# A two-block transformer in float32: first stage with x's high parts made by two engines, tile 1's statistics moved ahead of two weight parts, and tile 0's products issued in the order in which their operands are made

## The chip, the core and the metric

The kernel runs on one NeuronCore of a Trainium2 chip. The core has five engines that run apart from one another, each with its own instruction stream, and wait for each other by semaphores: TensorE (PE; its weight loads stand in the profile as PEld) multiplies matrices into PSUM; VectorE (DVE) and ScalarE (ACT) work on tiles in SBUF and PSUM; GpSimd (POOL) does a few small operations; SyncE (SP) issues most DMA transfers. The metric is the time of one execution on the device in microseconds (us), from one launch, with all inputs in the device's memory. Lower is better.

## What is computed

Two transformer blocks on 256 tokens of width 1024, all in float32. The change lies in the first lines of the first block:

```python
h = layer_norm(x, ln0_g, ln0_b)            # 256 x 1024
proj = h @ w_in[l] + b_in[l]               # 1024 x 4352
qa, ka, va, qb, kb, vb, ga, gb = jnp.split(proj, IN_SPLITS, axis=-1)
```

After it come neighbourhood attention and windowed attention, a gated mix, a feed-forward layer, and the second block with pooling, shared-key attention and two convolutional feed-forward layers.

## The kernel before

**Products in three pieces.** To keep float32 accuracy at the matmul's reduced-precision format, each operand is split into a high part (rounded to that format) and a low part (the remainder). A product is then three matmuls: high by high, low weight by high x, high weight by low x.

**Weights.** The class `Weights` streams 512 KB parts from memory in one fixed order. `load` (line 93) lets SyncE issue the transfer of the next part into one of six raw buffers (`wraw`). `high` (120) lets ScalarE write the high part (`whi`, line 134) and returns a function `low`; called, it lets VectorE write the low part (`wlo`, line 144) and then calls `load` for the next transfer, since the raw buffer is free after it. `highs(n)` (149) does n high parts and returns their `low` functions; `pump` (115) does both at once. Seven pairs of buffers hold split parts; `free` (161) gives a pair back.

**The first stage** (lines 505 to 591). The 256 tokens are two tiles of 128, `x_t[0]` and `x_t[1]`. `ln0(t)` (505) normalises a tile: two statistics instructions and their sum, then centring times the gain on VectorE (line 285), then the scaling by the inverse deviation, one half on ScalarE (`times`, line 341) and one on VectorE (514). `fm_banks` (347) transposes the tile with eight matmuls (line 354) into two PSUM banks of four 128-column pieces each. `parts0` (516) adds the layer norm's bias piece by piece and makes x's parts from the banks: eight high pieces `xh` (522), and, when the returned `lows` is called, eight low pieces `xl` (527), all on VectorE.

The first three 256-column units of `w_in` are two parts each, so parts 0 to 5. The class `Tm` multiplies them with the tokens as the stationary operand: `run(0)` (421) takes tile 0 through the three units, 24 matmuls each (line 434): high by high, low weight, low x, over eight pieces of x; the first unit takes the first four pieces of both high and low weight, then the other four, then low x. ScalarE evacuates each unit's sum (`tmc`, 439). Near the end of the last unit, `late` puts tile 1's transposes and its parts into the streams. `run(1)` then takes tile 1 through the same weights, frees them unit by unit, and splits a new part after each of the first two units. `finish` (444) transposes the results back (line 448), and the stages that follow go on with `unit_a` and others (mostly line 375).

**What sets the order.** The order on every engine is the order in which the program writes instructions; the scheduler is off. An engine works through its stream strictly, so an instruction that waits holds back everything behind it. On SyncE the loads stand in the order of the parts and each waits for the `low` that frees its raw buffer. The calls that set the order of the first stage are these:

```python
ln0(0)
bs = fm_banks(x_t[0])
lows = W.highs(2)
x_lows = parts0(bs, 0)
for low in lows:
    low()
x_lows()
```

After them come the transfer of the column constants `cols`, `W.pump(1)` three times (parts 2, 3, 4), `ln0(1)`, and `W.pump(2)` (parts 5, 6).

## Time and profile before

| | us |
|---|---|
| median of the runs shown | 869.26 |
| lowest run | 868.75 |
| the profiled execution | 869.44 |
| its span from the first to the last instruction | 867.7 |
| TensorE busy | 838.6 |
| VectorE busy | 642.3 |
| ScalarE busy | 489.9 |

The profile is of one execution. Its views are a page of totals, a table of chosen stretches of time, a timeline per engine, in which neighbouring instructions of one line are merged into one row (start, time from the first start to the last end, count), and a list of who waited for whom. A matmul's row carries the time until its last result is written, so rows that follow one another overlap; the pace is the distance between starts.

### The profile page before, as it was taken

Reading aid. Unit: us, or ns where it says so; the run is one execution under the profiler, and the core shown is the slowest. Engines: PE = TensorE matmul, PEld = TensorE weight load, DVE = VectorE, ACT = ScalarE, POOL = GpSimd, SP = SyncE. Lnnn points to the kernel's source line nnn. Section 1 sums busy time; section 2 is a strip of 40 time slices with the busy share of each in tenths; the row PEclk is TensorE's granted clock in tenths of the full one; section 3 lists DMA queues with packets and bytes.
Section 4 is the critical chain, followed back from the end, with each engine's and each line's share of the span. In section 5 each row is a group of like instructions: output and inputs, shape, how many; then the busy total and the mean of one; then the engine's idle time right before and its main releaser. Section 6 shows DMA issues by size and latency. Waiting matters only on the chain.

```text
span 867.7 us, 15201 instructions
## 1 busy us (share of the span) xinstructions
PE 838.6 (97%) x5874; PEld 758.8 (87%) x5874; DVE 642.3 (74%) x1145; ACT 489.9 (56%) x904; POOL 73.4 (8%) x97
## 2 busy tenths in 40 slices
PE   7999999999999999979999999999999999999997
PEld 5989889879889999879999999988776999999995
DVE  7575874786828888786799777664896689977772
ACT  3465666444624457455676655555785567665551
POOL 0003000002000000010000000138620000000000
PEclk9999999999999999999999999999999999999999
DMA  8494453558616666523557565434262456756531
GB/s 323 139 306 159 137 204 98 170 179 300 217 65 217 213 218 221 200 98 134 172 188 253 182 215 185 156 126 129 78 210 81 166 178 214 243 197 214 181 114 49
DMA packets 44042, 154.62 MB, mean 178 GB/s; under 512 B 5153, under 2 KB 6049, under 8 KB 43970
## 3 DMA queue, kind: packets, MB, share of 16 engines
q1 hardware_dynamic: 41616, 146.90, 49.6%
q0 software_dynamic: 1632, 5.93, 1.9%
q8 instruction: 46, 0.75, 0.3%
q10 hardware_dynamic: 722, 0.82, 0.3%
q14 instruction: 26, 0.21, 0.1%
HBM read 152.58 MB, written 1.05 MB: 177 GB/s over the span
## 4 chain that ended last, share of the span: by engine, by line
PE 39%; DVE 7%; ACT 6%; DMA 2%; issue 2%; POOL 1%; DVEq 0%; POOLq 0%; ACTq 0%
PE bank_a L375 22%; PE bank_b L375 13%; DVE wlo L144 2%; PE bank_a L434 2%; ACT whi L134 2%; DMA wraw<-wts_dram 2%; ACT p L1335 1%; ACT scr L308 1%; PE bank_a L1356 1%; DVE X L337 1%; DVE cv L1148 1%; POOL rstd L272 1%; PE bank_a L1242 0%; DVE p L741 0%; DVE cv L1146 0%
## 5 line engine op out<-in xcount | busy, mean ns | idle before, releaser
L144 DVE TENSOR_TENSOR wlo<-wraw,whi 128x1024 fp32r<-128x1024 f32 x261 | 312.2, 1225 | 74.3 <-ACT whi L134 73.7
L375 PE MATMUL bank_a<-xh,whi 128*128 128x256 f32 x1056 | 296.0, 280 | 1.9 <-DVE cv L1148 1.7
L375 PE MATMUL bank_a<-xh,wlo 128*128 128x256 f32 x1056 | 292.9, 277 | 0.6 <-DVE wlo L144 0.5
L375 PE MATMUL bank_a<-xl,whi 128*128 128x256 f32 x1056 | 292.8, 277 | 0.0
L134 ACT ACTIVATE whi<-wraw 128x1024 fp32r<-128x1024 f32 x261 | 264.9, 1050 | 19.2 <-DMA wraw<-wts_dram 16.5
L375 PEld LDWEIGHTS bank_a<-xh,whi 128*128 128x128 f32 x1056 | 198.6, 188 | 7.4 <-ACT whi L134 2.7
L375 PEld LDWEIGHTS bank_a<-xl,whi 128*128 128x128 f32 x1056 | 198.6, 188 | 1.7
L375 PEld LDWEIGHTS bank_a<-xh,wlo 128*128 128x128 f32 x1056 | 198.5, 188 | 1.0 <-DVE wlo L144 1.0
L1145 ACT ACTIVATE cv<-bank_a,cols 128x256 f32<-128x256 f32 x76 | 41.9, 558 | 79.0 <-PE bank_a L375 78.9
L375 PE MATMUL bank_b<-wlo,ah 128*128 128x512 f32 x176 | 69.4, 394 | 0.0
L375 PE MATMUL bank_b<-whi,al 128*128 128x512 f32 x176 | 69.0, 392 | 0.0
L375 PE MATMUL bank_b<-whi,ah 128*128 128x512 f32 x176 | 68.5, 389 | 0.0
L1146 DVE SCALAR_TENSOR_TENSOR cv<-bank_a,cols,cv 128x255 f32<-128x255 f32 x76 | 36.5, 480 | 42.1 <-ACT cv L1145 41.9
L375 PE MATMUL bank_b<-wlo,uh 128*128 128x512 f32 x128 | 50.4, 394 | 0.0
L375 PE MATMUL bank_b<-whi,ul 128*128 128x512 f32 x128 | 50.4, 393 | 0.0
L375 PE MATMUL bank_b<-whi,uh 128*128 128x512 f32 x128 | 50.0, 390 | 0.0
L344 ACT ACTIVATE uh<-ur 128x256 fp32r<-128x256 f32 x32 | 13.2, 412 | 59.1 <-DVE ur L942 44.1
L272 POOL TENSOR_TENSOR rstd<-ve,neghalf 128x1 f32<-128x1 f32 x22 | 13.4, 610 | 387.8 <-DVE ve L313 248.2
L921 POOL TENSOR_SCALAR wraw<-wraw,cols 128x256 f32<-128x256 f32 x28 | 29.8, 1082 | 165.8 <-DMA wraw<-wts_dram 162.9
L375 PEld LDWEIGHTS bank_b<-wlo,ah 128*128 128x128 f32 x176 | 33.1, 188 | 6.6
L1148 DVE SCALAR_TENSOR_TENSOR cv<-bank_a,cols,cv 128x254 f32<-128x254 f32 x76 | 36.6, 482 | 2.7
L375 PEld LDWEIGHTS bank_b<-whi,al 128*128 128x128 f32 x176 | 33.1, 188 | 6.3
(207 smaller groups left out, 1267.7 us busy)
## 6 DMA issues: line engine op xcount, KB each, us to landing
wraw<-wts_dram SPq DMA_DIRECT2D x268, 512.0 KB, 4.4
v<-bvec_dram POOLq DMA_DIRECT2D x10, 512.0 KB, 5.3
v<-bvec_dram SPq DMA_DIRECT2D x4, 512.0 KB, 8.0
nab<-nab_dram SPq DMA_DIRECT2D x4, 384.0 KB, 6.3
poolA<-const_dram POOLq DMA_DIRECT2D x1, 544.0 KB, 7.1
scr<-x_dram SPq DMA_DIRECT2D x2, 256.0 KB, 3.1
scr<-x_dram SPq DMA_DIRECT2D x1, 512.0 KB
out_dram<-X SPq DMA_DIRECT2D x2, 256.0 KB, 2.1
```

The lines of the kernel that those rows point to most:

```text
L134: self.nc.scalar.activation(out=hi, in_=r, func=AF.Copy)
L144: (eng or self.nc.vector).tensor_tensor(out=lo, in0=r, in1=hi.bitcast(F32), op=ALU.subtract)
L272: nc.gpsimd.tensor_tensor(out=r, in0=v, in1=neghalf, op=ALU.pow)
L308: nc.scalar.activation(out=junk[:, HALF[q if into is None else into]], in_=src, func=AF.Square, scale=1.0 / 32.0, accum_out=ss[:, q:q + 1])
L337: nc.vector.scalar_tensor_tensor(out=x[:, s], in0=junk[:, s], scalar=r, in1=x[:, s], op0=ALU.mult, op1=ALU.add)
L344: nc.scalar.activation(out=hi, in_=src, func=AF.Copy)
L375: nc.tensor.matmul(o, lhsT=l, rhs=r, start=start and i == 0, stop=stop and i == 2)
L434: nc.tensor.matmul(o[:, :256], lhsT=self.kx(k)[b][:, t * P:(t + 1) * P], rhs=self.cs[u][k // 4][a][:, k % 4, :], start=(i, k) == order[0], ...
L921: nc.gpsimd.tensor_scalar(out=d, in0=d, scalar1=g, scalar2=None, op0=ALU.mult)
L1145: nc.scalar.activation(out=v, in_=o[:, :T], func=AF.Identity, scale=col(c + 2), bias=col(c + 3))
L1146: nc.vector.scalar_tensor_tensor(out=v[:, 1:T], in0=o[:, 0:T - 1], scalar=col(c + 1), in1=v[:, 1:T], op0=ALU.mult, op1=ALU.add)
L1148: nc.vector.scalar_tensor_tensor(out=v[:, 2:T], in0=o[:, 0:T - 2], scalar=col(c), in1=v[:, 2:T], op0=ALU.mult, op1=ALU.add)
```

## The change

In `parts0` the high pieces can now be made by either engine: `act_high` on ScalarE, `high` on VectorE, and `low` on VectorE, each for a half of the pieces (`K0`: pieces 0 to 3, `K1`: 4 to 7). For tile 0 VectorE makes the high pieces of `K0` and ScalarE those of `K1`; for tile 1 it is the other way round. The low parts of the weights and of x alternate on VectorE. Tile 1's statistics come after the low part of weight part 2, ahead of the low part of 3; its centring and scaling come ahead of the low parts of 4 and 5, whose high parts are issued on ScalarE before tile 1's scaling. Tile 0's products are issued by `run0` in groups of four from a list of (unit, half, kind): kind 0 is high by high, 1 low weight, 2 low x. Tile 1's transposes stand ahead of the last two groups. Part 6 is split after them; the transfer of `cols` is issued behind tile 1's scaling and `halfb`, which reads it, later still. The computation is the same; only the order of the additions within a sum differs.

```diff
+            def run0(self, plan):
+                self.cs = [[W.take(4, 256) for _ in range(2)] for _ in range(self.n)]
+                o = [None] * self.n
+                left = [[(h, i) for h in range(2) for i in range(3)] for _ in range(self.n)]
+                for step in plan:
+                    if callable(step):
+                        step()
+                        continue
+                    u, h, i = step
...
+                    for k in range(4):
+                        nc.tensor.matmul(o[u][:, :256], lhsT=self.kx(4 * h + k)[b][:, 0:P],
+                                         rhs=self.cs[u][h][a][:, k, :], start=first and k == 0,
+                                         stop=not left[u] and k == 3)
+                    if not left[u]:
...
+                        nc.scalar.activation(out=self.tm[u][:, 0, :], in_=o[u][:, :256], func=AF.Copy)
...
+            def act_high(ks):
+                for k in ks:
+                    src, c, hi, _ = at(k)
+                    nc.scalar.activation(out=hi, in_=src, func=AF.Identity, bias=c)
...
         ln0(0)
-        bs = fm_banks(x_t[0])
-        lows = W.highs(2)
-        x_lows = parts0(bs, 0)
-        for low in lows:
-            low()
-        x_lows()
+        w_lows = W.highs(1)
+        act_high, high, low = parts0(fm_banks(x_t[0]), 0)
+        high(K0)
+        act_high(K1)
+        w_lows += W.highs(1)
+        w_lows[0]()
+        low(K0)
+        w_lows[1]()
+        low(K1)
+        w_lows += W.highs(1)
+        w_lows[2]()
+        w_lows += W.highs(1)
+        st = small([P, 2, 6], "bst")
+        for q in range(2):
+            ln_stats(x_t[1], st, q)
+        mr = ln_rstd(st)
+        w_lows[3]()
+        w_lows += W.highs(2)
+        ln_centre(x_t[1], mr, g0, 0)
+        times(x_t[1], mr[1], x_t[1], 0)
+        ln_centre(x_t[1], mr, g0, 1)
...
         nc.scalar.dma_start(out=cols[:, :C_B0], in_=cols_in[:, :C_B0])
-        for _ in range(3):
-            W.pump(1)
-        ln0(1)
-        W.pump(2)
...
-        tm.run(0, late=lambda: parts0(fm_banks(x_t[1]), 1)())
+        t1 = []
+
+        def tile1():
+            t1.extend(parts0(fm_banks(x_t[1]), 1))
+            t1[0](K0)
+            w_lows[4]()
+            w_lows[5]()
+            t1[1](K1)
+            for ks in (K0, K1):
+                t1[2](ks)
...
+        tm.run0([(0, 0, 0), (0, 0, 1), (0, 1, 0), (0, 0, 2), (0, 1, 1), (1, 0, 0), (0, 1, 2), (1, 0, 2), (1, 1, 0),
+                 (1, 1, 2), (1, 0, 1), (2, 0, 0), (2, 0, 2), (1, 1, 1), (2, 1, 0), (2, 1, 2), tile1,
+                 (2, 0, 1), (2, 1, 1)])
+        W.pump(1)
         tm.run(1, (2,))
```

**VectorE, from tile 0's high pieces to tile 1's parts.** Before; the numbers behind names are buffers: `wraw_94`, `96`, `98`, `101`, `103`, `105` are the raw weight parts 0 to 5, `scr_81` is tile 1.

```order
L527 SCALAR_TENSOR_TENSOR xl_116<-bank_a_130,cols_87,xh_115 128x128 x4
L527 SCALAR_TENSOR_TENSOR xl_116<-bank_a_135,cols_87,xh_115 128x128 x4
L144 TENSOR_TENSOR wlo_170<-wraw_98,whi_169 128x1024
L144 TENSOR_TENSOR wlo_176<-wraw_101,whi_175 128x1024
L144 TENSOR_TENSOR wlo_182<-wraw_103,whi_181 128x1024
L297 BN_STATS bst_187<-scr_81 128x6 x2
L278 BN_AGGR mv_190<-bst_187 128x2
L280 TENSOR_SCALAR ve_192<-mv_190 128x1
L285 SCALAR_TENSOR_TENSOR scr_81<-scr_81,mv_190,bank_b_107 128x512
L285 SCALAR_TENSOR_TENSOR scr_81<-scr_81,mv_190,bank_b_108 128x512
L514 TENSOR_SCALAR scr_81<-scr_81,rstd_194 128x512
L144 TENSOR_TENSOR wlo_201<-wraw_105,whi_200 128x1024
```

Now the same stretch, from the low part of weight part 0:

```order
L144 TENSOR_TENSOR wlo_131<-wraw_94,whi_130 128x1024
L555 SCALAR_TENSOR_TENSOR xl_116<-bank_a_133,cols_87,xh_115 128x128 x4
L144 TENSOR_TENSOR wlo_152<-wraw_96,whi_151 128x1024
L555 SCALAR_TENSOR_TENSOR xl_116<-bank_a_138,cols_87,xh_115 128x128 x4
L144 TENSOR_TENSOR wlo_169<-wraw_98,whi_168 128x1024
L297 BN_STATS bst_177<-scr_81 128x6 x2
L278 BN_AGGR mv_180<-bst_177 128x2
L280 TENSOR_SCALAR ve_182<-mv_180 128x1
L144 TENSOR_TENSOR wlo_175<-wraw_101,whi_174 128x1024
L285 SCALAR_TENSOR_TENSOR scr_81<-scr_81,mv_180,bank_b_107 128x512
L285 SCALAR_TENSOR_TENSOR scr_81<-scr_81,mv_180,bank_b_108 128x512
L582 TENSOR_SCALAR scr_81<-scr_81,rstd_184 128x512
```

The statistics of tile 1 (`bst`) stand behind the low part of weight part 2 instead of behind that of 4, and tile 1's centring has the low parts of 0 to 3 ahead of it where it had those of 0 to 4. The low parts of 4 and 5 are the next two rows.

**ScalarE, the same stretch.** Before:

```order
L134 ACTIVATE whi_140<-wraw_94 128x1024
L134 ACTIVATE whi_143<-wraw_96 128x1024
L538 DMA cols_87<-cols_dram 128x440
L134 ACTIVATE whi_169<-wraw_98 128x1024
L134 ACTIVATE whi_175<-wraw_101 128x1024
L134 ACTIVATE whi_181<-wraw_103 128x1024
L341 ACTIVATE scr_81<-scr_81,rstd_194 128x512
L134 ACTIVATE whi_200<-wraw_105 128x1024
L134 ACTIVATE whi_206<-wraw_155 128x1024
```

and now:

```order
L134 ACTIVATE whi_130<-wraw_94 128x1024
L545 ACTIVATE xh_115<-bank_a_138,cols_87 128x128 x4
L134 ACTIVATE whi_151<-wraw_96 128x1024
L134 ACTIVATE whi_168<-wraw_98 128x1024
L134 ACTIVATE whi_174<-wraw_101 128x1024
L134 ACTIVATE whi_189<-wraw_103 128x1024
L134 ACTIVATE whi_192<-wraw_105 128x1024
L341 ACTIVATE scr_81<-scr_81,rstd_184 128x512
L584 DMA cols_87<-cols_dram 128x440
L441 ACTIVATE tmc_230<-bank_a_200 128x256
```

Four high pieces of x stand between the high parts of weight parts 0 and 1. The high part of 5 (`wraw_105`) stood behind tile 1's scaling (`scr_81`) and stands ahead of it; the transfer of `cols` stood behind the high part of 1 and stands behind the scaling.

**TensorE, the second half of tile 0's products and tile 1's transposes.** Before, `whi_169` to `wlo_176` are parts 2 and 3, `181`, `200`, `201` parts 4 and 5:

```order
L434 MATMUL bank_a_241<-whi_175,xh_115 128x256 x4
L434 MATMUL bank_a_241<-wlo_170,xh_115 128x256 x4
L434 MATMUL bank_a_241<-wlo_176,xh_115 128x256 x4
L434 MATMUL bank_a_241<-whi_169,xl_116 128x256 x4
L434 MATMUL bank_a_241<-whi_175,xl_116 128x256 x4
L434 MATMUL bank_a_268<-whi_181,xh_115 128x256 x4
L434 MATMUL bank_a_268<-whi_200,xh_115 128x256 x4
L434 MATMUL bank_a_268<-wlo_182,xh_115 128x256 x4
L434 MATMUL bank_a_268<-wlo_201,xh_115 128x256 x4
L434 MATMUL bank_a_268<-whi_181,xl_116 128x256 x2
L354 MATMUL bank_a_287<-ident_86,scr_81 128x128 x4
L354 MATMUL bank_a_292<-ident_86,scr_81 128x128 x4
```

and now, with `168`, `169`, `174`, `175` for parts 2 and 3 and `189` to `193` for 4 and 5:

```order
L436 MATMUL bank_a_221<-whi_174,xh_115 128x256 x4
L436 MATMUL bank_a_221<-whi_174,xl_116 128x256 x4
L436 MATMUL bank_a_221<-wlo_169,xh_115 128x256 x4
L436 MATMUL bank_a_248<-whi_189,xh_115 128x256 x4
L436 MATMUL bank_a_248<-whi_189,xl_116 128x256 x4
L436 MATMUL bank_a_221<-wlo_175,xh_115 128x256 x4
L436 MATMUL bank_a_248<-whi_192,xh_115 128x256 x4
L436 MATMUL bank_a_248<-whi_192,xl_116 128x256 x4
L354 MATMUL bank_a_271<-ident_86,scr_81 128x128 x4
L354 MATMUL bank_a_276<-ident_86,scr_81 128x128 x4
L436 MATMUL bank_a_248<-wlo_190,xh_115 128x256 x4
L436 MATMUL bank_a_248<-wlo_193,xh_115 128x256 x4
```

The groups with low parts of the third unit's weights stood ahead of tile 1's transposes and are now the only ones behind them; the groups of the second and the third unit take turns.

## Rows read from the trace of the kernel before

**Rows 1.** The page, busy us (share of the span) xinstructions of each engine.

```profile
PE 838.6 (97%) x5874; PEld 758.8 (87%) x5874; DVE 642.3 (74%) x1145; ACT 489.9 (56%) x904; POOL 73.4 (8%) x97
```

**Rows 2.** Stretches: busy us per engine, granted clock, DMA share, GB/s.

```profile
12.00:16.00 4.00, 4.00 (x20) 4.00 (x21) 4.00 (x10) 2.12 (x2) 0.00 (x0) 1.00 1.02 406
...
20.00:22.50 2.50, 0.00 (x0) 0.00 (x0) 1.88 (x4) 1.68 (x3) 0.55 (x1) 1.00 0.78 305
22.50:26.00 3.50, 3.45 (x16) 3.45 (x17) 2.45 (x3) 1.48 (x3) 0.00 (x0) 0.51 0.36 90
26.00:38.00 12.00, 12.00 (x97) 11.43 (x96) 6.68 (x18) 4.20 (x9) 0.00 (x0) 1.00 0.34 113
38.00:50.00 12.00, 12.00 (x83) 10.54 (x82) 7.42 (x10) 7.25 (x14) 0.00 (x0) 1.00 0.79 248
50.00:60.00 10.00, 10.00 (x60) 8.28 (x59) 7.84 (x8) 6.89 (x10) 0.00 (x0) 1.00 0.90 290
```

**Rows 3.** Timeline of TensorE: start us, us, what xcount [idle before <-releaser].

```profile
7.41 1.97 PE L354 MATMUL bank_a<-ident,scr 128*128 128x128 f32 x8 [0.21 <-ACT scr L341]
...
9.29 1.22 PE L434 MATMUL bank_a<-whi,xh 128*128 128x256 f32 x4
...
11.91 1.22 PE L434 MATMUL bank_a<-wlo,xh 128*128 128x256 f32 x4 [1.40 <-DVE wlo L144]
...
22.55 1.22 PE L434 MATMUL bank_a<-whi,xh 128*128 128x256 f32 x4 [3.02 <-ACT whi L134]
...
23.57 1.91 PE L434 MATMUL bank_a<-wlo,xh 128*128 128x256 f32 x8
...
25.27 0.63 PE L434 MATMUL bank_a<-whi,xl 128*128 128x256 f32 x2
...
33.82 1.10 PE L434 MATMUL bank_a<-whi,xh 128*128 128x256 f32 x8
...
36.65 1.07 PE L448 MATMUL bank_a<-ident,tmc 128*128 128x128 f32 x8
```

**Rows 4.** Timeline of VectorE, the same columns.

```profile
8.56 2.16 DVE L522 TENSOR_SCALAR xh<-bank_a,cols 128x128 fp32r<-128x128 f32 x8 [0.77 <-PE bank_a L354]
...
10.63 2.35 DVE L144 TENSOR_TENSOR wlo<-wraw,whi 128x1024 fp32r<-128x1024 f32 x2
...
12.90 2.15 DVE L527 SCALAR_TENSOR_TENSOR xl<-bank_a,cols,xh 128x128 fp32r<-128x128 f32 x8
...
14.97 3.49 DVE L144 TENSOR_TENSOR wlo<-wraw,whi 128x1024 fp32r<-128x1024 f32 x3
...
18.38 1.28 DVE L297 BATCH_NORM_STATS2 bst<-scr 128x6 f32<-128x512 f32 x2
...
20.00 1.39 DVE L285 SCALAR_TENSOR_TENSOR scr<-scr,mv,bank_b 128x512 f32<-128x512 f32 x2
...
21.50 0.49 DVE L514 TENSOR_SCALAR scr<-scr,rstd 128x512 f32<-128x512 f32 x1
```

**Rows 5.** Timeline of ScalarE, the same columns.

```profile
8.17 1.06 ACT L134 ACTIVATE whi<-wraw 128x1024 fp32r<-128x1024 f32 x1 [0.82 <-DMA wraw<-wts_dram]
...
13.21 1.06 ACT L134 ACTIVATE whi<-wraw 128x1024 fp32r<-128x1024 f32 x1 [1.48 <-DMA wraw<-wts_dram]
...
14.87 1.07 ACT L134 ACTIVATE whi<-wraw 128x1024 fp32r<-128x1024 f32 x1 [0.61 <-DMA wraw<-wts_dram]
...
20.82 0.72 ACT L341 ACTIVATE scr<-scr,rstd 128x512 f32<-128x512 f32 x1 [4.88 <-DVE scr L285]
...
37.84 0.85 ACT L565 ACTIVATE fm_ka<-bank_a,cols 128x256 f32<-128x256 f32 x2
...
40.68 0.47 ACT L565 ACTIVATE fm_ka<-bank_a,cols 128x256 f32<-128x256 f32 x1
```

**Rows 6.** SyncE's longest wait to 130 us; a stretch in the middle.

```profile
SPq L100 <- DVE wlo L144: 82.8, 26, 8.5
...
387.00:392.00 5.00, 4.97 (x30) 4.73 (x28) 4.38 (x5) 1.54 (x3) 0.55 (x1) 0.66 0.09 37
```

More of the change, by code (lines that the diff above doesn't have):

```diff
@@ L516, in parts0, with at @@
         def parts0(bs, t):
-            todo = []
-            for k in range(8):
-                src = bs[k // 4][:, k % 4 * P:(k % 4 + 1) * P]
-                hi, lo = (a[:, k, t * P:(t + 1) * P] for a in xT)
-                nc.vector.tensor_scalar(out=hi, in0=src, scalar1=col(C_B0 + k), scalar2=None, op0=ALU.add)
-                todo.append((lo, src, col(C_B0 + k), hi))
-            def lows():
-                for lo, src, c, hi in todo:
+            def at(k):
+                return (bs[k // 4][:, k % 4 * P:(k % 4 + 1) * P], col(C_B0 + k)) + tuple(
+                    a[:, k, t * P:(t + 1) * P] for a in xT)
@@ L527, in lows, with high, low @@
+            def act_high(ks):
+                for k in ks:
+                    src, c, hi, _ = at(k)
+                    nc.scalar.activation(out=hi, in_=src, func=AF.Identity, bias=c)
+            def high(ks):
+                for k in ks:
+                    src, c, hi, _ = at(k)
+                    nc.vector.tensor_scalar(out=hi, in0=src, scalar1=c, scalar2=None, op0=ALU.add)
+            def low(ks):
+                for k in ks:
+                    src, c, hi, lo = at(k)
                     nc.vector.scalar_tensor_tensor(out=lo, in0=src, scalar=c, in1=hi.bitcast(F32), op0=ALU.add,
@@ L528, in lows @@
                                                    op1=ALU.subtract)
[L529 removed]
+            return act_high, high, low
+        K0, K1 = range(4), range(4, 8)
         ln0(0)
[L532 to L537 removed]
+        w_lows = W.highs(1)
[3 more added lines that the diff above has]
+        w_lows += W.highs(1)
@@ new lines, in model @@
+        w_lows[0]()
[14 more added lines that the diff above has]
+        ln_centre(x_t[1], mr, g0, 1)
+        nc.vector.tensor_scalar(out=x_t[1][:, HALF[1]], in0=x_t[1][:, HALF[1]], scalar1=mr[1], scalar2=None,
+                                op0=ALU.mult)
@@ L555, in load_nab @@
             nc.sync.dma_start(out=nab[p], in_=nab_in[p])
-        halfb = few.tile([P, 16], F32, name="halfb")
-        nc.vector.tensor_scalar(out=halfb, in0=cols[:, C_GA:C_GA + 16], scalar1=0.5, scalar2=None, op0=ALU.mult)
         fm = {}
@@ L591, in model @@
         tm.finish(1, qk_epi(("ka0", "ka1"), (C_KA, C_KA + 1)))
+        halfb = few.tile([P, 16], F32, name="halfb")
+        nc.vector.tensor_scalar(out=halfb, in0=cols[:, C_GA:C_GA + 16], scalar1=0.5, scalar2=None, op0=ALU.mult)
         W.pump(1)
```

14 lines of the change are left out of this document (8 added, 6 removed).

## The prediction, made before the changed kernel was run

> **What bounds the kernel now.** I read the page's busy table first: TensorE is busy 97% of the span [rows 1], so time is won only where TensorE waits or runs slowly. The table of stretches shows such a place: no matmul from 20.0 to 22.5, then 3.5 us at a granted clock of 0.51, and from 26 on TensorE busy without a gap through 60 us [rows 2]. TensorE's timeline of the first 38 us gives the waits: 1.40 us until 11.91 for `wlo`, 3.02 us until 22.55 for `whi` [rows 3]. It also gives the pace. Eight products took 1.70 us (23.57 to 25.27), 0.2125 each, where the granted clock is the lower level; 24 took 2.83 us (33.82 to 36.65), 0.118 each, at the upper one. The four products at 11.91 took 1.22 us, just as long as the four at 22.55 under the low clock, although the granted column says 1.00 from 12 to 16 [rows 2]: I trust the pace, and with 20 products in those 4 us (0.2 each, near the lower pace) I read the clock as low until about 15.8. So the stage that ends at 36.65 (the transposes of line 448) holds 144 products and 16 transposes, about 19 us of work at the upper pace, and took from 7.41 to 36.65.
>
> Who is late? VectorE's timeline [rows 4] is a chain without a pause from 8.56 to 21.99: high parts of x, two `wlo`, low parts, three `wlo`, then all of tile 1's layer norm. ScalarE waits behind it: it scales tile 1 at 20.82 and only then turns to `whi` of part 5, which the third unit needs. That turn is the 3.02 us wait.
>
> **The change, step by step.** Everything until 8.56 stays. I walk VectorE's new order with spacings from [rows 4]: an `xh` or `xl` of 128x128 is 0.259 (2.07 us from 12.90 to 14.97 for eight), a `wlo` 1.135 (2.27 us from 10.63 to 12.90 for two), the statistics until the centring 1.62 (18.38 to 20.00), the two centrings 1.50 (20.00 to 21.50), the scaling 0.49.
>
> - Four `xh` from 8.56 to 9.59, `wlo` 0 to 10.73, four `xl` to 11.76, `wlo` 1 to 12.90, four `xl` to 13.93, `wlo` 2 to 15.07.
> - Statistics to 16.69, `wlo` 3 to 17.82, centring to 19.32, scaling to 19.81, `wlo` 4 to 20.95, and `wlo` 5, now the last part that the stage needs, ends 1.23 later at 22.18.
>
> ScalarE must keep ahead of that chain. `whi` 0 runs 8.17 to 9.23 [rows 5]; the transposes end at 9.38 [rows 3]; then come its four `xh`, an operation of this size that the trace doesn't have on ScalarE. The nearest row is the 128x256 one with a bias: two took 0.85, one 0.47 [rows 5], 0.38 apart. Bounds are 0.19 (half the columns, half the time) and 0.38 (no less for fewer columns); I take 0.26, taking off 128 columns at the pace of `whi` (1.06 us for 1024, 0.12). Four end at 9.43 + 1.04 = 10.47, `whi` 1 at 11.53, ahead of 11.76 when VectorE wants it. At 0.38 it ends at 12.01: 0.25 us late. At 0.19 nothing changes, since VectorE decides.
>
> One sentence of the Trainium skill speaks against this edit: the page "ScalarE: Activation LUTs", section "Rules for kernel authors", gives adds to VectorE rather than ScalarE, and its section "What ACT_TABLE_LOAD costs" prices an activation with a pointer bias at about 280 ns + 0.833 ns a column with some 93 ns of overlap, an estimated 0.29 apart for 128 columns. By the page's price `whi` 1 would end at about 11.65, still in time, and the sum would be the same; no row of before has that size.
>
> The later weights are no limit: part 3 landed at 13.21 and part 4 at 14.87 [rows 5] and are wanted at 16.69 and 19.81. Part 5 has no row; at 406 GB/s [rows 2] its 0.524 MB takes 1.3 us behind part 4, so `whi` 5 ends near 17.3, wanted at 20.95. The `cols` transfer, now issued behind tile 1's scaling at about 19.3, is wanted by `halfb` and the bias reads near 30.
>
> TensorE then. After the first four products (over by 10.5) it waits for `wlo` 0 until 10.79, and from there the groups of four stand in the order in which parts arrive. At the lower pace a group is 0.85, at the upper one 0.47. With the rise at 15.8 the six groups from 10.79 reach 15.8 and the next ten and eight transposes about 21.1; each group's data is older than its turn (`xl` at 13.93 for a group at 15; `wlo` 3 at 17.88 for one at 18.8; tile 1 scaled by 19.81 for transposes from 20.2). `wlo` 4 lets four more go by 21.6, and TensorE waits some 0.6 us for `wlo` 5, until 22.18 + 0.06 (the step from `wlo` to matmul: 10.63 + 1.22 = 11.85 against 11.91). From 22.24 there are 4 + 72 products left. Their inputs are ahead: tile 1's `xh` halves are made by ScalarE until about 21.8 and by VectorE until 23.2, the last `xl` at 25.25, when TensorE is at its twentieth product after the start, at 24.6, with 8 to run. So 76 x 0.118 = 8.97, and the line-448 transposes start at 31.21 instead of 36.65: 5.44 us earlier.
>
> After that the order on every engine is the old one. ScalarE's `whi` and VectorE's `wlo` of later parts stand behind the same evacuations, each a little earlier, and SyncE's next loads are set off by the `wlo` [rows 6], so they move along. Sum: the profiled execution took 869.44 (its span 867.7), so 869.44 - 5.44 = **864.0 us**. The median shown, 869.26, is 0.18 lower than that execution; the difference is inside the noise. The gain is 0.6%; a measurement of this kernel tells about 2% from no change.
>
> **Uncertain inside this case.** If the clock rises 3.4 us later (the length of the low stretch in [rows 2]), TensorE and not VectorE decides: from 10.79, 148 pieces remain (140 products, 8 transposes); 8.4 us at 0.2125 make 39.5 of them, 108.5 at 0.118 end at 32.0, a gain of 4.6, 864.8. ScalarE's upper price adds 0.25. An earlier rise gives nothing, because `wlo` 5 decides. Own range: 863.6 to 865.2.
>
> **Rivals.** (a) *The gain is absorbed behind the stage by the weight stream.* For it: DMA share 0.79 and 0.90 from 38 to 60 [rows 2]. If that stream can't start earlier, TensorE waits later: back to 869.4 if all goes, 866.7 if half. Against: from 26 to 38 the share was only 0.34 [rows 2]; SyncE waited 82.8 us on `wlo` in the first 130 us [rows 6], that is for buffers, not bandwidth; and TensorE is fully busy from 38 to 60.
>
> (b) *Another low-clock stretch appears or the one in the middle goes.* From 387 to 392 the mean granted clock is 0.66 [rows 6], so 3.4 of 5 us were low. Everything there comes 5.4 us earlier. Without it: 1.7 us less, 862.3. With one more: 865.7. The Trainium skill's page "TensorE: Matmul & The Clock Gate", section on the HAM clock gate, says that the monitor runs free and does not restart with the kernel, so that the moment of a change differs between executions; one execution can't show it.
>
> (c) *Slower: TensorE stays at 1.2 GHz through the stage*, because products now come in fours as parts arrive. For it: the clock fell after the 3.02 us wait [rows 2, 3], and VectorE's parts for tile 0 are spread over 13.6 us (8.56 to 22.18). Price: 10.79 + 148 x 0.2125 = 42.2 against 36.65, 5.6 later, 875. It decides if the rise comes later than about 29.6: there the formula 0.118 x 148 + 0.555 x 10.79 + 0.445 T reaches 36.65. Against: waits after 10.79 add up to about 0.6 us; before, the clock rose while the products ran on from 11.91, and rose again at 26 while they ran on from 22.55.
>
> **Chances.** The forecast 0.74; (b) without the middle stretch 0.07, with one more 0.07; (a) 0.09, spread from 865 to 869.4; (c) 0.03. The range 861.9 to 867.0 leaves out (c), the worse half of (a) and a rest of the others, some 0.12. None of the cases passes 2% (851.9 or 886.6): faster 0.01, same 0.98, slower 0.01.
>
> **What would show it.** Right: `wlo` 5 ends near 22.2; no idle stretch of TensorE over 1 us after 10.8; the upper pace from about 16 without a fall near 22.6; the line-468 transposes (448 before) start near 31.2; TensorE stays full to 60. Wrong: ScalarE's four `xh` over 0.4 us each; `whi` 3 or 5 ending after VectorE's turn at 16.7 or 20.95 (a weight that lands late); the pace 0.2125 behind 19; new waits for `whi` or for a load between 31 and 60; or idle time of TensorE after 60 that before did not have.

## The result: 863.2 us, with the gain in the stage where it was expected

| | before | after |
|---|---|---|
| median of the comparison's runs, us | 869.89 | 863.23 |
| lowest, highest run of after, us | | 862.20, 864.72 |
| the profiled execution, us | 869.44 | 862.61 |
| its span, us | 867.7 | 860.8 |
| start of the transposes that end the first stage, us | 36.65 | 31.12 |
| span behind that point, us | 831.0 | 829.7 |

The ratio is 0.9935, with a 95% interval of 0.9915 to 0.9954. Forecast were 864.0 us (861.9 to 867.0) and "within 2%"; both held. The median of before is that of four runs, one of which took 2369.59 us; the other three lie between 868.75 and 870.52. Of the 6.8 us between the two profiled spans 5.53 lie in the first stage (forecast: 5.44), and 1.3 behind it, where the program is the old one.

The page of the changed kernel, busy us by engine, hardly differs from [rows 1], since most of what went was waiting: of the 6.9 us between the spans TensorE loses 5.3 of idle and 1.6 of busy time.

```profile
PE 837.0 (97%) x5874; PEld 757.2 (88%) x5874; DVE 640.0 (74%) x1137; ACT 491.8 (57%) x912; POOL 74.3 (9%) x97
```

The stretches of [rows 2], and two for [rows 6] (us, then busy us of TensorE, its weight loads, VectorE, ScalarE, GpSimd, then granted clock, DMA share, GB/s):

```profile
20.00:22.50 2.50, 2.10 (x17) 1.82 (x17) 2.50 (x5) 1.14 (x4) 0.00 (x0) 1.00 0.75 265
22.50:26.00 3.50, 3.50 (x32) 3.50 (x31) 3.50 (x12) 1.67 (x4) 0.00 (x0) 1.00 0.71 256
26.00:38.00 12.00, 12.00 (x104) 11.78 (x104) 5.14 (x6) 6.65 (x13) 0.00 (x0) 1.00 0.67 203
...
375.00:383.00 8.00, 6.34 (x40) 5.95 (x41) 5.41 (x10) 6.69 (x15) 1.65 (x3) 0.79 0.19 66
387.00:392.00 5.00, 5.00 (x43) 4.87 (x43) 3.95 (x7) 2.20 (x6) 0.55 (x1) 1.00 0.70 220
```

From 20.0 to 22.5 TensorE had no matmuls, now it has 17; from 22.5 to 26 the clock was 0.51 with 16 matmuls, now it is 1.00 with 32. The weights come earlier (DMA share 0.67 instead of 0.34 from 26 to 38).

TensorE's timeline (start us, us, what, xcount, and in brackets the idle time before it and what ended it):

```profile
10.76 1.22 PE L436 MATMUL bank_a<-wlo,xh 128*128 128x256 f32 x4 [0.55 <-DVE wlo L144]
...
15.19 1.25 PE L436 MATMUL bank_a<-whi,xl 128*128 128x256 f32 x8
16.28 0.63 PE L436 MATMUL bank_a<-whi,xh 128*128 128x256 f32 x4
...
20.93 0.74 PE L436 MATMUL bank_a<-wlo,xh 128*128 128x256 f32 x4
22.06 0.74 PE L436 MATMUL bank_a<-wlo,xh 128*128 128x256 f32 x4 [0.40 <-DVE wlo L144]
...
31.12 1.07 PE L468 MATMUL bank_a<-ident,tmc 128*128 128x128 f32 x8
```

Against [rows 3]: the wait of 3.02 us is gone; two waits for `wlo` are left, 0.55 and 0.40. Groups of four stand 0.85 apart until about 15 and 0.47 apart from 16.28 on. The last four products of tile 0 start at 22.06; they and the 72 of tile 1 take 9.06 us to the transposes.

VectorE's and ScalarE's timelines and GpSimd's one row, for [rows 4, 5]:

```profile
8.45 1.13 DVE L550 TENSOR_SCALAR xh<-bank_a,cols 128x128 fp32r<-128x128 f32 x4 [0.77 <-PE bank_a L354]
...
16.60 1.23 DVE L144 TENSOR_TENSOR wlo<-wraw,whi 128x1024 fp32r<-128x1024 f32 x1
17.74 1.40 DVE L285 SCALAR_TENSOR_TENSOR scr<-scr,mv,bank_b 128x512 f32<-128x512 f32 x2
19.25 0.49 DVE L582 TENSOR_SCALAR scr<-scr,rstd 128x512 f32<-128x512 f32 x1
19.65 2.35 DVE L144 TENSOR_TENSOR wlo<-wraw,whi 128x1024 fp32r<-128x1024 f32 x2
```

```profile
9.30 1.14 ACT L545 ACTIVATE xh<-bank_a,cols 128x128 fp32r<-128x128 f32 x4 [1.11 <-PE bank_a L354]
10.31 3.05 ACT L134 ACTIVATE whi<-wraw 128x1024 fp32r<-128x1024 f32 x3
...
14.84 1.06 ACT L134 ACTIVATE whi<-wraw 128x1024 fp32r<-128x1024 f32 x1 [0.20 <-DMA wraw<-wts_dram]
```

```profile
16.75 1.49 POOL L272 TENSOR_TENSOR rstd<-ve,neghalf 128x1 f32<-128x1 f32 x1 [10.36 <-DVE ve L280]
```

VectorE has no pause from 8.45 to 22.00 (19.65 + 2.35), the end of `wlo` 5, so no weight came too late for it. ScalarE has made the last high part by 15.90, long before VectorE wants it.

That the gain is carried on shows in waits which both kernels have, deep in the program. Behind one for `gb` TensorE goes on at 160.69 (before: 166.56), 5.87 us earlier. For one late in the program here is TensorE's row of the changed kernel, and then that of the kernel before:

```profile
706.39 0.36 PE L375 MATMUL bank_a<-xh,whi 128*128 128x256 f32 x1 [0.54 <-DVE cv L1205]
```

```profile
712.93 0.36 PE L375 MATMUL bank_a<-xh,whi 128*128 128x256 f32 x1 [0.77 <-DVE cv L1148]
```

6.54 us earlier: nothing of the stage's 5.53 is given back.

### The profile page after: what moved, and what is told of

Its sections match the earlier page's. It is cut to its first block, busy times and chain, and to the rows that moved or that the text cites. A ratio compares the mean times of both kernels' runs of the same rounds, so it can differ in the third digit from the quotient of the medians.

```text
span 860.8 us, 15204 instructions
## 1 busy us (share of the span) xinstructions
PE 837.0 (97%) x5874; PEld 757.2 (88%) x5874; DVE 640.0 (74%) x1137; ACT 491.8 (57%) x912; POOL 74.3 (9%) x97
## 4 chain that ended last, share of the span: by engine, by line
PE 42%; ACT 7%; DVE 6%; issue 2%; DMA 1%; POOL 0%; DVEq 0%; POOLq 0%; ACTq 0%
PE bank_a L375 22%; PE bank_b L375 15%; PE bank_a L454 2%; ACT whi L134 2%; DVE wlo L144 2%; DMA wraw<-wts_dram 1%; ACT p L1392 1%; ACT scr L308 1%; PE bank_a L1413 1%; PE bank_a L354 1%; DVE cv L1205 1%; PE bank_a L1299 0%; DVE cv L1203 0%; DVE X L337 0%; POOL rstd L272 0%
## 5 line engine op out<-in xcount | busy, mean ns | idle before, releaser
L134 ACT ACTIVATE whi<-wraw 128x1024 fp32r<-128x1024 f32 x261 | 264.7, 1050 | 16.9 <-DMA wraw<-wts_dram 14.1
```

The source lines that it names most:

```text
L134: self.nc.scalar.activation(out=hi, in_=r, func=AF.Copy)
```

## The experiments

The start of x's high parts differs between executions (8.14 to 9.41 us over fourteen profiles), so the stage is counted from there. "Chain" is the time from that start to the end of the low part of 5, "stage" the time to the transposes of the results, both from the profiled execution; "rest" is the span behind. Ratios are to the kernel before in the same call.

| kernel | chain | stage | rest | median us | ratio, 95% interval |
|---|---|---|---|---|---|
| before | 15.19 | 28.09 | 831.0 | 869.26 / 868.96 / 869.66 / 868.81 | |
| after | 13.56 | 22.67 | 829.7 | 863.23 | 0.9935 [0.9915, 0.9954] |
| e1 high parts all on VectorE | 14.59 | 24.45 | 830.4 | 865.91 | 0.9959 [0.9933, 0.9984] |
| e2b old order of products | 13.55 | 24.49 | 829.5 | 865.46 | 0.9956 [0.9934, 0.9977] |
| e3 statistics late | 13.54 | 22.65 | 828.9 | 864.20 | 0.9926 [0.9895, 0.9957] |
| e8 before + sharing | 14.96 | 28.28 | 833.2 | 868.01 | 0.9991 [0.9970, 1.0012] |
| e10 before + sharing, alternating | 14.16 | 25.22 | 829.9 | 866.18 | 0.9964 [0.9941, 0.9986] |
| e5 VectorE longer | 14.74 | 25.38 | 838.5 | 873.75, one execution | |
| e6 TensorE longer | 13.56 | 22.95 | 834.8 | 868.26, one execution | |
| e4 before + products in the wait | 15.19 | 26.84 | 836.0 | 872.97 | 1.0031 [1.0006, 1.0056] |
| e7 low part of 4 on GpSimd | 13.56 | 23.14 | 831.6 | 864.88 | 0.9956 [0.9940, 0.9971] |
| e9 low part of 3 on GpSimd | 12.39 | 21.43 | 832.7 | 864.10 | 0.9933 [0.9910, 0.9956] |
| f1 after, again | 13.55 | 22.67 | 829.7 | 863.75 | 0.9941 [0.9920, 0.9961] |
| f2 e9's kernel, again | 14.18 | 23.30 | 830.2 | 862.79 | 0.9920 [0.9894, 0.9946] |

The theory, from the prediction (V in the expectations): VectorE's chain up to `wlo` 5 decides when TensorE can go on, and TensorE's old end follows it. The rivals: TensorE's own work decides (P), or a lower clock (C), or the weights' arrival.

### One part of the change undone

**e1: no sharing of the high parts.**

```diff
-        act_high(K1)
+        high(K1)
...
-            t1[0](K0)
             w_lows[4]()
             w_lows[5]()
+            t1[1](K0)
             t1[1](K1)
```

> The changed kernel with all of x's high pieces made by VectorE again (both tiles); nothing else moved. Theory V (VectorE's chain up to the low part of weight part 5 sets when TensorE can finish tile 0): four pieces of 0.259 more stand ahead of that part, so it ends at 23.0 instead of 22.0, and eight instead of four stand between it and tile 1's low pieces. Tile 1's last low piece is then done at 27.1 and the first unit of tile 1 ends at 27.3 instead of 25.5: stage end 33.0 against 31.1, time 1.9 us over the changed kernel. Rival P (TensorE's own pace and order set it, the pieces are hidden): less than 0.5 us.

The chain is 1.03 us longer, exactly four high pieces, and the stage 1.78. The other 0.75 us stand behind `wlo` 5: VectorE then makes all eight of tile 1's high pieces alone, and the eight products that use them, 0.94 us elsewhere, run at its pace:

```profile
24.64 1.88 PE L454 MATMUL bank_a<-whi,xh 128*128 128x256 f32 x8
26.36 1.10 PE L454 MATMUL bank_a<-wlo,xh 128*128 128x256 f32 x8
```

The eight took 1.72 (24.64 to 26.36), 0.78 more. (The low-x products behind them lose another 0.18, and the last six groups win 0.2 back, since they run at the shorter of the two distances told of at the end.) So the sharing is worth 1.8 us when the rest of the change is there, 1.0 for tile 0 and 0.75 for tile 1. (The stage's end was 33.86 instead of the expected 33.0, since x came 0.96 us later in this execution.)

**e2b: the old order of the products.**

```diff
-        tm.run0([(0, 0, 0), (0, 0, 1), (0, 1, 0), (0, 0, 2), (0, 1, 1), (1, 0, 0), (0, 1, 2), (1, 0, 2), (1, 1, 0),
-                 (1, 1, 2), (1, 0, 1), (2, 0, 0), (2, 0, 2), (1, 1, 1), (2, 1, 0), (2, 1, 2), tile1,
-                 (2, 0, 1), (2, 1, 1)])
+        tm.run0([(0, 0, 0), (0, 0, 1), (0, 1, 0), (0, 1, 1), (0, 0, 2), (0, 1, 2),
+                 (1, 0, 0), (1, 1, 0), (1, 0, 1), (1, 1, 1), (1, 0, 2), (1, 1, 2),
+                 (2, 0, 0), (2, 1, 0), lows45, (2, 0, 1), (2, 1, 1), tile1, (2, 0, 2), (2, 1, 2)])
```

> The changed kernel with tile 0's products in the order of before (per unit: high by high, low weight, low x; tile 1's transposes behind the low-weight groups of the third unit); the other engines as in the changed kernel. Theory V: the low part of weight part 5 still ends at 22.0, but now the transposes (0.9) stand behind its products, so tile 1's pieces start 1.5 us later on VectorE; stage end 32.7, 1.6 us over the changed kernel. Rival P (the order in which products are issued is the main thing): TensorE waits for each low part in turn and the low clock comes back; more than 3 us of the 5.5 lost.

The chain is the same to 0.01 us, the stage 1.82 longer. TensorE waits for parts while it has others to work on, and has them still to do when the last part comes:

```profile
18.09 0.74 PE L436 MATMUL bank_a<-wlo,xh 128*128 128x256 f32 x4 [1.85 <-DVE wlo L144]
...
22.27 0.74 PE L436 MATMUL bank_a<-wlo,xh 128*128 128x256 f32 x4 [0.40 <-DVE wlo L144]
22.85 1.03 PE L354 MATMUL bank_a<-ident,scr 128*128 128x128 f32 x8
23.64 1.19 PE L436 MATMUL bank_a<-whi,xl 128*128 128x256 f32 x8
24.66 1.10 PE L454 MATMUL bank_a<-whi,xh 128*128 128x256 f32 x8
```

Eight transposes and eight products, 1.81 us (22.85 to 24.66), now stand behind `wlo` 5; in the changed kernel they stood ahead of it. Rival P falls: the clock did not come down behind the wait of 1.85 us (the next four took 0.74 us), and less than 3 us were lost.

**e3: tile 1's statistics behind parts 3 and 4.**

```diff
+        w_lows[3]()
+        w_lows += W.highs(2)
+        w_lows[4]()
         st = small([P, 2, 6], "bst")
...
         mr = ln_rstd(st)
-        w_lows[3]()
-        w_lows += W.highs(2)
         ln_centre(x_t[1], mr, g0, 0)
```

> The changed kernel with tile 1's statistics behind the low parts of weight parts 3 and 4 instead of ahead of them (its centring and scaling follow at once, ahead of the low part of 5). Theory V: the same work stands ahead of the low part of 5, which ends at 22.0 as before; tile 1 is scaled at 20.8 instead of 19.7, its transposes end at 21.5, still ahead of the wait; stage end 31.1, time within 0.3 us of the changed kernel. Rival S (the place of the statistics is what the change lives on): at least 1.3 us (their duration) lost, stage end 32.4 or later.

Nothing lost: 22.65 against 22.67. TensorE waits for tile 1 instead of for a weight part, and what came earlier for it lies behind:

```profile
20.36 1.17 PE L354 MATMUL bank_a<-ident,scr 128*128 128x128 f32 x8 [0.82 <-ACT scr L341]
21.28 1.40 PE L436 MATMUL bank_a<-wlo,xh 128*128 128x256 f32 x8
```

All of this is ahead of `wlo` 5 in either order, so the chain's length is the same, and rival S falls. Where the statistics stand among parts 3 and 4 is worth nothing; that all of the normalisation stands ahead of 5 is not touched by this run.

### One part of the change alone

**e8: the kernel before, with the sharing only.**

```diff
-                nc.vector.tensor_scalar(out=hi, in0=src, scalar1=col(C_B0 + k), scalar2=None, op0=ALU.add)
+                if (k >= 4) == (t == 0):
+                    nc.scalar.activation(out=hi, in_=src, func=AF.Identity, bias=col(C_B0 + k))
+                else:
+                    nc.vector.tensor_scalar(out=hi, in0=src, scalar1=col(C_B0 + k), scalar2=None, op0=ALU.add)
...
-        lows = W.highs(2)
+        lows = W.highs(1)
         x_lows = parts0(bs, 0)
+        lows += W.highs(1)
```

> The kernel before with one part of the change alone: half of x's high pieces on ScalarE (tile 0's second half, tile 1's first half). Theory V: VectorE's chain to tile 1's scaling is 1.03 shorter, so the high part of weight part 5 and with it the wait of TensorE end 1.03 earlier (21.5), and tile 1's low pieces come up to 1.03 earlier again; stage end between 35.6 (clock falls as before) and 34.0 (it does not). Rival P: nothing, 36.6.

My expectation failed. VectorE had 1.03 us less to do, and the chain was 0.23 shorter. The row that says why:

```profile
11.71 1.23 DVE L144 TENSOR_TENSOR wlo<-wraw,whi 128x1024 fp32r<-128x1024 f32 x1 [0.71 <-ACT whi L134]
```

The high part of weight part 1 stands on ScalarE behind its four pieces of x; VectorE, which in the old order takes `wlo` 0 and 1 one behind the other, waits 0.71 us for it. That puts the rest of the chain 0.80 us back, and 0.23 of the 1.03 is left. TensorE's wait of 3.02 us was there as before, and the lower clock lasted longer in this execution (its products are at the upper pace again from 28.54 on, in the kernel before from 26.64), so that 13.32 us lie between `wlo` 5 and the end of the stage instead of 12.90, and the stage was no shorter. How much of this is the execution's clock, one profile doesn't tell; the median's ratio, 0.9991, shows no gain either.

**e10: the same, with the low parts alternating as in the changed kernel.**

```diff
-        for low in lows:
-            low()
-        x_lows()
+        for i, low in enumerate(lows):
+            low()
+            x_lows(slice(4 * i, 4 * i + 4))
```

> The kernel before with x's high pieces shared by two engines, and with the low parts alternating on VectorE as in the changed kernel (low part of weight part 0, four low pieces of x, low part of 1, four low pieces of x); tile 1's statistics and the order of the products stay as before. With the sharing alone VectorE stood 0.71 us still for the high part of weight part 1, which ScalarE makes behind its four pieces, and the chain behind it was no earlier than before. Theory W (that wait ate the gain): with four low pieces of x in the place of the wait VectorE doesn't stop, the low part of 2 ends 6.5 us after the start of x's high parts (7.5 to 7.6 in the kernel before and with the sharing alone), tile 1's normalisation and the wait for the high part of 5 come 1.0 us earlier, and the stage takes 27.0 us instead of 28.0, or 25.5 if the clock stays up through the shorter wait. Rival D (the weights' arrival holds VectorE): waits for a high part appear ahead of the low part of 2 or 3, and the stage stays at 28.

W holds: VectorE doesn't stop, the low part of 2 ends 6.6 us after the start (expected 6.5), the chain is 14.16, 1.03 shorter than before, and TensorE's wait falls from 3.02 to 1.66:

```profile
21.38 0.74 PE L434 MATMUL bank_a<-whi,xh 128*128 128x256 f32 x4 [1.66 <-ACT whi L134]
```

The product behind it starts at the upper pace (0.74 us for four, 1.22 in [rows 3]): the clock stayed up, and the stage is 25.2, as was expected for that case (25.5). Rival D falls, since no wait for a weight stands in VectorE's chain. So the gain adds up from parts that need one another: the sharing alone gave 0.23 us on VectorE's chain and nothing on the stage, with alternation 2.87: 1.03 on the chain, and 1.84 behind `wlo` 5, of which e4 below puts 1.25 on the clock; 0.6 are left, for which tile 1's high pieces, shared here too, are the likely cause. The rest, up to 5.42, comes from the order of the products and of tile 1's work.

### Which engine decides

**e5: VectorE longer**, two more statistics instructions ahead of `wlo` 5.

```diff
             w_lows[4]()
+            st2 = small([P, 2, 6], "bst")
+            for q in range(2):
+                ln_stats(x_t[1], st2, q)
             w_lows[5]()
```

> The changed kernel with two more statistics instructions on VectorE (a copy that nobody reads, 1.2 us) between the low parts of weight parts 4 and 5. Theory V: the stage ends 1.2 us later, at 32.3. Rival P: less than 0.4 us later, since TensorE is behind anyway.

The chain is 1.18 longer, as expected, but the stage 2.71, 1.5 more than expected. The surplus is the clock:

```profile
22.93 0.80 PE L436 MATMUL bank_a<-wlo,xh 128*128 128x256 f32 x4 [1.58 <-DVE wlo L144]
23.53 1.91 PE L454 MATMUL bank_a<-whi,xh 128*128 128x256 f32 x8
25.24 1.85 PE L454 MATMUL bank_a<-wlo,xh 128*128 128x256 f32 x8
26.92 1.10 PE L454 MATMUL bank_a<-whi,xl 128*128 128x256 f32 x8
```

Sixteen products took 3.39 us (23.53 to 26.92) instead of 1.88: 1.51, and 1.18 + 1.51 = 2.69. VectorE decides; and in this execution the clock fell behind a wait of only 1.58 us.

**e6: TensorE longer**, eight more products ahead of the last group.

```diff
-                 (2, 0, 1), (2, 1, 1)])
+                 (2, 0, 1), filler, (2, 1, 1)])
```

> The changed kernel with 8 products more on TensorE (into a bank that nobody reads, 0.94 us) ahead of the last group of tile 0, where TensorE waits 0.4 to 0.6 us for the low part of weight part 5. Theory V: the wait takes in part of it, stage end 31.5. Rival P (TensorE sets the stage): 0.94 us later, 32.1.

0.94 us of work (21.76 to 22.70) made the stage 0.28 longer; the other 0.66 went into the time that TensorE waits for `wlo` 5. In the changed kernel that time is 22.06 - 20.93 - 0.47 = 0.66. P (all of it added) falls.

### The clock in the kernel before

**e4: the kernel before, with 24 products in the wait of 3.02 us.**

```diff
+                        if late and u == self.n - 1 and i == 0 and k == 4:
+                            spare2 = ps.tile([P, 512], F32, tag="b_2", name="spare2", bufs=1)
+                            for j in range(24):
+                                nc.tensor.matmul(spare2[:, :256], lhsT=self.kx(j % 4)[0][:, 0:P],
+                                                 rhs=self.cs[u][0][0][:, j % 4, :], start=j == 0, stop=j == 23)
```

> The kernel before with 24 products more on TensorE (into a bank that nobody reads) in its 3.02 us wait for the high part of weight part 5; nothing else changed. Theory V: if the granted clock then stays up, the pace is 0.118 from 22.55 on, tile 1's transposes start at 24.5 instead of 25.7 and VectorE's pieces at 25.0 instead of 26.5; stage end 35.1, 1.5 us of the 5.5 and no more, since VectorE's chain is as it was. Rival C (the gain of the change is the clock that no longer falls): 3 us or more. If the clock falls in spite of the products: stage end 36.65.

In the stage it came as expected: the chain is that of before, the clock stays at 1.00 and the stage is 1.25 shorter, with work added.

```profile
19.15 2.99 PE L435 MATMUL spare<-whi,xh 128*128 128x256 f32 x24
22.34 0.74 PE L439 MATMUL bank_a<-whi,xh 128*128 128x256 f32 x4 [0.19 <-ACT whi L134]
```

The median, though, is above that of before (872.97 against 868.96). The edit's condition was also true in two later stages, which I had overlooked; the record of that line shows 72 products instead of 24 (name, xcount: ns of one, first and last start us):

```profile
L435 PE MATMUL spare<-whi,xh x72: 278/280/281, 19.2 to 685.6; 128*128 128x256 f32 x72
```

48 x 0.118 = 5.7 us of work behind the stage, where the rest is 5.0 longer. So the time of this kernel says nothing on the clock; its stage does: of the 5.4 us, about a quarter (1.25) is the lower clock behind the 3.02 us wait. Rival C (3 us or more) falls.

### A version with GpSimd

**e7: the low part of weight part 4 on GpSimd**, with the last two groups swapped.

```diff
-            w_lows[4]()
+            w_lows[4](nc.gpsimd)
...
-                 (2, 0, 1), (2, 1, 1)])
+                 (2, 1, 1), (2, 0, 1)])
```

> The changed kernel with the low part of weight part 4 made by GpSimd instead of VectorE, and the two last groups of tile 0 swapped so that part 5 comes first. Theory V: VectorE's chain is 1.13 shorter, part 5 ends at 20.9 and tile 1's pieces start at 20.9. If GpSimd needs 3 us from 18.2 on, part 4 is there at 21.2 and the stage ends at 30.5, 0.6 us under the changed kernel, now with TensorE as the bound; if it needs over 4 us, or if VectorE is slowed by it, the stage ends later than 31.1. Rival P: no gain whatever GpSimd needs.

GpSimd took only 2.39 us, and nothing was gained: the chain is 13.56, as without it.

```profile
18.48 2.39 POOL L144 TENSOR_TENSOR wlo<-wraw,whi 128x1024 fp32r<-128x1024 f32 x1
```

```profile
18.01 1.40 DVE L285 SCALAR_TENSOR_TENSOR scr<-scr,mv,bank_b 128x512 f32<-128x512 f32 x2
19.52 1.63 DVE L582 TENSOR_SCALAR scr<-scr,rstd 128x512 f32<-128x512 f32 x1
```

The scaling, 0.49 us elsewhere, took 1.63 and ended 0.28 after GpSimd's instruction (20.87); the centring beside it kept its 1.40. The 1.13 us taken off VectorE were spent waiting for GpSimd. The stage is 0.47 longer, and that comes from the swap of the two groups. TensorE's rows:

```profile
21.29 0.63 PE L354 MATMUL bank_a<-ident,scr 128*128 128x128 f32 x4 [0.69 <-ACT xh L545]
22.33 1.21 PE L436 MATMUL bank_a<-wlo,xh 128*128 128x256 f32 x8 [0.41 <-DVE wlo L144]
```

The second four of tile 1's transposes wait 0.69 us (the scaling that they read ended at 21.15), but TensorE then waits again, for `wlo` 5, so this costs nothing. Behind `wlo` 5 there now stand both groups, eight products, where the changed kernel had four: 9.53 us from 22.33 to the end of the stage at 31.86 instead of 9.06, four products of 0.118 more. The low part of 4 had been ready since 20.87 (18.48 + 2.39). The run therefore doesn't tell V from P; e9 does.

**e9: the low part of 3 on GpSimd**, ahead of the statistics, so that it runs beside statistics and centring.

```diff
+        w_lows[3](nc.gpsimd)
         st = small([P, 2, 6], "bst")
...
         mr = ln_rstd(st)
-        w_lows[3]()
```

> The changed kernel with the low part of weight part 3, instead of part 4, on GpSimd, written ahead of tile 1's statistics. In the run with part 4 on GpSimd that instruction took 2.39 us there (18.48 to 20.87), and VectorE's scaling of tile 1, 0.49 us elsewhere, took 1.63 beside it (19.52 to 21.15), so that the 1.13 us saved on VectorE came back at once. Theory H (the scaling waited for GpSimd; statistics and centring, which read one operand from SBUF or take one from PSUM, do not): GpSimd works while VectorE does the statistics and the centring, both keep their length (1.28 for the two statistics, 1.40 for the two centrings), the scaling takes 0.49, and the low part of 5 ends 1.1 us earlier than in the changed kernel, counted from the start of x's high parts: 12.4 instead of 13.56 after it; TensorE then has almost no wait left and the stage (from the start of x's high parts to the transposes of the results) takes about 21.7 us instead of 22.6. Theory G (anything VectorE does beside GpSimd slows): statistics and centring stretch by the 1.1 us, the low part of 5 ends at 13.5 again and the stage takes 22.6 or more.

H holds: the statistics took 1.28, the centring 1.40, the scaling 0.49, the chain is 12.39 (expected 12.4) and the stage 21.43 (expected 21.7). VectorE's chain is 1.17 shorter and the stage 1.24, so the chain still decides, and P falls.

```profile
14.67 1.28 DVE L297 BATCH_NORM_STATS2 bst<-scr 128x6 f32<-128x512 f32 x2
...
16.30 1.40 DVE L285 SCALAR_TENSOR_TENSOR scr<-scr,mv,bank_b 128x512 f32<-128x512 f32 x2
17.80 0.49 DVE L582 TENSOR_SCALAR scr<-scr,rstd 128x512 f32<-128x512 f32 x1
```

The median didn't show it, so the changed kernel (f1) and this one (f2) were run again, side by side.

> The changed kernel once more, unaltered, on the same chip as the next run, so that the two can be compared. In its first profile the stage, from the start of x's high parts to the transposes of the results, took 22.6 us and the rest of the program 829.7; over ten profiles of this study's kernels the rest varied between 828.9 and 838.5 without the program behind the stage having changed. Theory N (that variation is the execution's and not the kernel's): median 863 to 865, the stage again 22.6 +-0.3, the rest anywhere from 829 to 838. Theory K (the rest belongs to the kernel): the rest again within 0.5 us of 829.7.

> The changed kernel with the low part of weight part 3 on GpSimd, ahead of tile 1's statistics, unaltered from the earlier run, in which the stage took 21.3 us instead of 22.6 and ended 1.5 us earlier, while the median (864.1) lay no lower than the changed kernel's. Theory N (the gain of the stage is carried to the end, the variation of the rest hid it): the stage takes 21.3 +-0.3 again, and the median lies 1.0 to 1.5 us below that of the changed kernel in this call. Theory A (the gain is absorbed behind the stage): the stage is as short, the medians within 0.4 us, and a new wait or a wait that is longer by about a microsecond stands somewhere behind the stage in every profile of this kernel and in none of the changed one.

f1 repeats the changed kernel to 0.01 us in the chain. f2 doesn't repeat e9 (its stage was 21.43; the expectation of f2 says 21.3). The two fences are VectorE's and GpSimd's rows of f2; the third is GpSimd's row of e9:

```profile
14.03 3.00 DVE L144 TENSOR_TENSOR wlo<-wraw,whi 128x1024 fp32r<-128x1024 f32 x1
```

```profile
13.56 2.39 POOL L144 TENSOR_TENSOR wlo<-wraw,whi 128x1024 fp32r<-128x1024 f32 x1 [7.45 <-ACT whi L134]
```

```profile
14.07 2.96 POOL L144 TENSOR_TENSOR wlo<-wraw,whi 128x1024 fp32r<-128x1024 f32 x1 [8.17 <-ACT whi L134]
```

In f2 the high part was ready at 13.56, GpSimd began ahead of VectorE's `wlo` 2, and that took 3.00 us instead of 1.22, until 1.08 after GpSimd's end. In e9 VectorE was 0.5 us ahead, and GpSimd waited. The same kernel is 1.2 us better than the changed one or 0.6 worse in the stage, depending on which of the two reaches that point first. The medians, 862.79 and 863.75, don't separate the kernels (their intervals overlap). Whether e9's gain is carried to the end was not tested, since the stage wasn't shorter in f2's profile. The rest of f1, 829.7, would fit K as well as N; that of this one kernel, 832.7 in e9 and 830.2 in f2, speaks for N: it varies with the execution (mostly by the distance of products, told of at the end). I don't call this a better version.

## Why the prediction was right

**Start and durations.** x's high parts start at 8.45 (8.56 in [rows 4]). ScalarE's four `xh`, the one operation that had no row, stand 0.253 apart (9.30 to 10.31 for four), where I had taken 0.26 between bounds of 0.19 and 0.38. The estimate of 0.29 from the Trainium skill, page "ScalarE: Activation LUTs", section "What ACT_TABLE_LOAD costs", is above the rows, and the measurement decides. The rule of the same page of the Trainium skill, section "Rules for kernel authors", that gives adds to VectorE rather than ScalarE doesn't fit here: at 0.25 against 0.26 a piece the two engines are equal, and VectorE was the one that was waited for (e1: 1.8 us).

**VectorE's walk.** `wlo` 5 ends at 22.00, forecast 22.18; the chain is 13.56 against 13.62 in the forecast. The steps were met: `wlo` 3 at 17.83 (17.82), the centring ahead of the scaling without a pause, `wlo` 4 ahead of the last group.

**The weights.** Part 5's high part ended at 15.90, not near 17.3: the estimate from the GB/s of the stretch was 1.4 us late. It changed nothing, since VectorE wants the part at 20.8.

**TensorE.** The wait for `wlo` 5 was put at 0.6; it is 0.66 (e6). The 76 products behind it were put at 8.97 us; they took 9.06. Sum 31.21, measured 31.12: 5.53 us earlier instead of 5.44, of which 0.11 is the earlier start in this execution. What I priced without naming it is that the lower clock of [rows 2] is part of the gain; e4 puts it at 1.25 us, and sixteen products at the lower level cost e5 1.51. Two things in the walk were not as written. The "next ten" groups are nine by the list of products; the 21.1 us go by nine, so the sum stands. And the rise of the clock at 15.8, met here (0.85 a group until 15, 0.47 from 16.28), is the execution's and was luck: in e9 the four products at 10.46 already took 0.74 us. It changes nothing, as the prediction says, because `wlo` 5 decides.

**The rivals.** (a) did not come: SyncE waited less for `wlo` in the first 130 us than in [rows 6], the DMA share from 26 to 38 went from 0.34 to 0.67, and the marks above are reached 5.87 and 6.54 us earlier.

```profile
SPq L100 <- DVE wlo L144: 71.8, 24, 8.2
```

(b) did not come: from 387 to 392 the clock is now 1.00, but from 375 to 383 it is 0.79, so, the column being a mean of 1.00 and 0.50, 8 x 0.21 x 2 = 3.4 us at the lower level, as long as before and 10 us earlier. (c) did not come in the changed kernel; e5 shows how near it is: with 1.18 us more on VectorE the clock fell for sixteen products, in the one execution that there is.

**What the forecast didn't hold.** 1.3 us of the profiled difference lie outside the stage. The program there is unaltered, and the rest of one and the same kernel was 832.7 and 830.2 in two executions (e9, f2), so I put no cause to it. The distance of products told of below is not it: by the count given there it costs 7.0 us over 0.1131 a step in both profiles. TensorE's idle time behind the stage is 1.4 us less (15.5 before, 14.1 after), but in f1, whose rest is 829.7 too, it is 15.0. That the median, 863.23, lies 0.8 under the forecast says nothing on the mechanism: the repeat, f1, has 863.75, 5.1 under before in its call.

**The parts.** The prediction walked the whole change and had no price for a single part. The runs give them: order of the products 1.8, sharing 1.8 in the changed kernel and, without alternating low parts, nothing on the stage of its one profile (e8), place of the statistics 0. One part was never run by itself, ScalarE's high part of 5 ahead of tile 1's scaling. Its price can be read from VectorE's row in the kernel before, behind [rows 4]:

```profile
22.53 2.36 DVE L144 TENSOR_TENSOR wlo<-wraw,whi 128x1024 fp32r<-128x1024 f32 x2 [0.54 <-ACT whi L134]
```

VectorE waited 0.54 us for that part, inside the chain. Counted from the start of x's high parts the stage is 5.42 us shorter, 1.63 in the chain and 3.79 behind it. The chain loses four high pieces (1.03) and this wait (0.54), 1.57; behind it the order of the products (e2b, 1.82), the clock (e4, 1.25) and tile 1's shared pieces (e1, 0.75) make 3.82. The sums fit, but the terms come from runs on two different kernels, and e8 shows that a part can be worth less by itself.

## What to carry to other kernels

Write down the chain of the engine that is waited for, instruction by instruction, and let everything else only keep ahead of it: a sum of twelve steps was right to 0.1 us here. Give the waiting engine its work in the order in which the inputs come, so that as little as possible is left when the last one arrives; and when work goes to a second engine, look at what stands behind it there (e8 lost 0.8 of 1.03 us to one high part); and when two groups change places, look at how many products then stand behind the last part (e7's swap cost 0.47 us). An engine of the side, such as GpSimd, is only free beside instructions that don't make it or the other wait, and whether they do can hang on half a microsecond.
